# Two projections side by side, rope tables and squared sums on DVE, and shifted due times in a two-block Transformer kernel

## The chip, the core and the metric

The kernel runs on one core of a Trainium2 chip. The metric is the device time of one execution in microseconds (us). PE is the matrix engine (TensorE), DVE the vector engine (VectorE), ACT the scalar engine (ScalarE), POOL is GpSimd, SP the engine that issues most of the DMAs.

## The reference

The input is one sequence of 256 tokens of width 1024, in fp32. Two blocks follow each other.

The first block puts 16 meta tokens ahead of the sequence (272 tokens), normalizes (RMS), projects, runs two kinds of attention, and then a gated FFN of width 2816. Cut to what matters here:

```python
h = rms_norm(x, attn_norm_g)
qa, ka, va, qb, kb, vb = split(h @ w_in)     # A: 8 query heads, 2 key heads of 64; B: 4 x 2 heads
qa = apply_rope(rms_norm(qa, a_q_norm_g), ang_a)
ka = apply_rope(rms_norm(ka, a_k_norm_g), ang_a)
out_a = softmax(qa ka^T / 8) va
out_b = rms_norm((softmax_0 - lam * softmax_1) vb, subln_g)
x = x + concat(out_a, out_b) @ w_out
x = x + (silu(h2 @ w_gate) * (h2 @ w_up)) @ w_down
```

The second block has a gated spatial MLP, a dilated window attention in three groups, a merge of both, and an FFN of width 4096 with a squared ReLU. The change touches its instructions only through the planner's order.

## The kernel before

**Precision by splitting.** Every fp32 operand of a matmul is held as two parts, `hi` (rounded to fp32r) and `lo` (the rest), and a product is made of three matmuls: hi x hi, hi x lo, lo x hi. ACT writes `hi` with a copy, DVE writes `lo` with a subtraction. Weights come as chunks of 128x1024 fp32 (512 KB) in the order of use. `Weights` loads them into four raw buffers (`wraw`), splits them into six pairs `whi`, `wlo` (`fill`, one ACT copy and one DVE subtraction for each chunk, called a chunk split below; the first chunk is split in two halves of 512 columns), and issues the next load behind each split. The hidden state of the first block is `hx` (128 partitions, 8 slices of 128 features, hi and lo, 272 tokens), made at the start from `xT`, the transposed input: for each slice k an ACT copy scaled by the norm's gain column and a DVE multiply-and-subtract.

**Projections of the first block.** There are 18 (`P1`, each through `proj`): kA, qA0, vA, qA1 to qA3, and k, q, v of the four B heads. One takes one chunk: for each k two matmuls (whi with hi and lo of `hx`), then eight with wlo. With q and k follow a square on ACT (for the norm), and `rotate`: a shuffle and a product with a cosine table on DVE, a product with a sine table on POOL, an addition on DVE. The eight tables (cos and sin for q and k of A and B, 128x272 each) are rope values times gain columns, made at the start by eight POOL `tensor_scalar` instructions. `token_sums` adds up the squares of x over the slices (seven POOL additions of 128x272) and makes from them the terms of the norms (`msx`, `emx`, `rx`). Powers of -1/2 run on POOL. Then come scores, softmax, transposes and products with v (`SA`, `TA`, `VA`, `SB`, `TB`, `VB`), and the output projection (`WO`).

**The order of the work.** `Recorder` doesn't issue at once. It notes each instruction with its dependences and a price in ns (`price`), and `flush` runs a list scheduler over them: each engine takes, of the instructions that are ready, the one with the earliest due time. Due times come from a target per PE instruction, handed back through the dependences. Six rounds are made, each with the times of the one before as targets, and the order with the earliest end of PE is issued. Each engine then runs its queue in this fixed order. There are two flushes: one after the first block's FFN has reached feature tile f6, one at the end. As all instructions are issued in `flush`, the profile gives all of them line 422.

**The start.** PE runs nine warm-up matmuls on zeros. SP issues the loads in the order of `FIRST`: x slices 0 and 1, `cols` (34 columns, among them the eight gain columns of the norm), the first chunk's first half, x slices 2 and 3, its second half, the rest of x, then chunks, `ind`, `rope`, `ident`, `lam`.

Of the kernel before, what the change touches and what calls it, by code (L numbers as in the profile page):

```python
# [19 lines left out]
T = 256  # L20
# [201 lines left out]
ISSUE, FETCH, LAND = 470.0, 1100.0, 950.0  # L222
# [4 lines left out]
def late(a, b):  # L227
    return LAND if a == "sync" else LATE.get((a, b), 150.0)
# [6 lines left out]
class Recorder:  # L235


    def __init__(self, tc, nc):
        self.tc, self.nc = tc, nc
        self.ops, self.acc, self.label, self.next = [], {}, "", set()  # L240
        self.clock = {e: 0.0 for e in ("tensor", "vector", "scalar", "gpsimd", "sync")}

    def engine(self, name):
        rec, eng = self, getattr(self.nc, name)

        class Proxy:
# [4 lines left out]

    def add(self, eng, m, fn, args, kw):
# [11 lines left out]
        o.cost = self.price(eng, m, outs, ins, kw)  # L264
# [43 lines left out]
    def price(self, eng, m, outs, ins, kw):  # L308
# [35 lines left out]
        return 100.0 + 1.43 * n * int(list(outs[0].ap)[0][1]) / 128.0  # L344

    def schedule(self, target):
# [16 lines left out]
        moved, bank = 0.0, {}  # L363
# [3 lines left out]
        while len(order) < len(ops):  # L367
# [29 lines left out]
            for j in o.succ:  # L397
                ready[j] = max(ready[j], clock[e] if e == ops[j].eng == "sync" else end + late(e, ops[j].eng))
# [5 lines left out]
    def flush(self):  # L404
# [45 lines left out]
class Weights:  # L450
# [56 lines left out]
def build(tc, a, out):  # L507
# [7 lines left out]
    V, S, G, PE, DMA = (R.engine(n) for n in ("vector", "scalar", "gpsimd", "tensor", "sync"))  # L515
# [11 lines left out]
    cols = top.tile([128, 34], F32, name="cols")  # L527
# [4 lines left out]
    hx = top.tile([128, 8, 2, L], F32R, name="hx")  # L532
# [176 lines left out]
    xT = prob[:, : 8 * L].rearrange("p (k q) -> p k q", k=8)  # L709
# [13 lines left out]
    for step in FIRST:  # L723
        R.follow()
        if step[0] == "x":
            ks = slice(int(step[1]), int(step[2]))
            DMA.dma_start(xT[:, ks], a["xT"][:, ks])
        elif step == "c":
            DMA.dma_start(cols, a["cols"])
        elif step == "w":  # L730
            W.load()
        else:
            W.load_part(int(step[1]))
    R.follow()
    DMA.dma_start(ind, a["ind"])
    R.follow()
    DMA.dma_start(rope, a["rope1"])
    R.follow()
    DMA.dma_start(ident, a["ident"])
    R.follow()  # L740
    DMA.dma_start(lamv, bass.AP(tensor=a["lam"].tensor, offset=a["lam"].offset, ap=[[0, 128], [64, 4], [1, 64]]))
# [880 lines left out]
```

## Time and profile before

| | |
|---|---|
| median of 3 runs | 739.33 us (738.82 to 739.93) |
| the profiled execution | 738.85 us, its span 737.1 us |
| granted clock of PE, mean | 0.992 of 2.4 GHz |
| busy share of PE, DVE, ACT, POOL | 98%, 73%, 59%, 9% |
| read from HBM | 130 MB, 178 GB/s over the span |

The span runs from the first instruction to the last. Busy times count instructions at work, not waits; a matmul's end is modelled, so neighbours overlap in the rows, and the distance from start to start is the better measure. The granted clock is a share of 2.4 GHz: 1.00 is the upper level, 0.50 the lower one of 1.2 GHz. A row of a timeline merges like instructions that follow each other; in brackets stands how long the engine had idled before, and what ended it.

### The profile page before, as it was taken

Reading aid. Unit: us, or ns where it says so; the run is one execution under the profiler, and the core shown is the slowest. Engines: PE = TensorE matmul, PEld = TensorE weight load, DVE = VectorE, ACT = ScalarE, POOL = GpSimd, SP = SyncE. Lnnn points to the kernel's source line nnn. Section 1 sums busy time; section 2 is a strip of 40 time slices with the busy share of each in tenths; the row PEclk is TensorE's granted clock in tenths of the full one; section 3 lists DMA queues with packets and bytes.
Section 4 is the critical chain, followed back from the end, with each engine's and each line's share of the span. In section 5 each row is a group of like instructions: output and inputs, shape, how many; then the busy total and the mean of one; then the engine's idle time right before and its main releaser. Section 6 shows DMA issues by size and latency. Waiting matters only on the chain.

```text
span 737.1 us, 11095 instructions
## 1 busy us (share of the span) xinstructions
PE 723.6 (98%) x4085; PEld 625.3 (85%) x4085; DVE 539.0 (73%) x944; ACT 431.3 (59%) x779; POOL 67.9 (9%) x81
## 2 busy tenths in 40 slices
PE   8989999999999999999999999999999999999996
PEld 5989988888888888888888889888888888888885
DVE  6897986666666665678748999757999766666663
ACT  6697775655555545466646766656656544454441
POOL 5932230100000000010000000000130000000000
PEclk8999999999999999999999999999999999999998
DMA  8553314466865565547655444545646755555621
GB/s 286 166 194 122 136 58 144 143 204 229 296 197 182 191 196 195 181 142 255 215 187 177 157 153 138 171 159 191 194 149 192 251 190 195 194 190 189 197 89 57
DMA packets 37639, 131.85 MB, mean 179 GB/s; under 512 B 4432, under 2 KB 5200, under 8 KB 37584
## 3 DMA queue, kind: packets, MB, share of 16 engines
q1 hardware_dynamic: 37584, 131.14, 53.8%
q8 instruction: 32, 0.52, 0.3%
q14 instruction: 23, 0.19, 0.1%
HBM read 130.07 MB, written 1.05 MB: 178 GB/s over the span
## 4 chain that ended last, share of the span: by engine, by line
PE 89%; DVE 5%; ACT 3%; issue 1%; DMA 1%; SPq 0%; POOLq 0%; POOL 0%; DVEq 0%; ACTq 0%
PE bank L422 89%; DVE wlo L422 2%; ACT prob L422 1%; DVE tiny L422 1%; DMA prob<-in_xT_dram 1%; ACT whi L422 1%; DVE ro L422 0%; DVE ptl L422 0%; DVE qkf L422 0%; DVE rr L422 0%; ACT hx L422 0%; DVE q L422 0%; ACT L422 0%; ACT vhiA L422 0%; SPq L422 0%
## 5 line engine op out<-in xcount | busy, mean ns | idle before, releaser
L422 DVE TENSOR_TENSOR wlo<-wraw,whi 128x1024 fp32r<-128x1024 f32 (+1 forms) x235 | 286.9, 1225 | 117.6 <-ACT whi L422 115.6
L422 ACT ACTIVATE whi<-wraw 128x1024 fp32r<-128x1024 f32 (+1 forms) x235 | 245.3, 1052 | 126.9 <-issue 73.4
L422 PE MATMUL bank<-hx,whi 128*128 128x512 f32 (+2 forms) x1152 | 270.2, 370 | 3.7 <-DVE ptl L422 1.1
L422 PEld LDWEIGHTS bank<-hx,whi 128*128 128x128 f32 x1152 | 196.2, 190 | 34.8 <-ACT whi L422 1.9
L422 PE MATMUL bank<-whi,mix 128*128 128x512 f32 x496 | 154.9, 392 | 0.0
L422 PEld LDWEIGHTS bank<-hx,wlo 128*128 128x128 f32 x1008 | 136.7, 189 | 9.5
L422 PE MATMUL bank<-hx,wlo 128*128 128x256 f32 (+1 forms) x1008 | 141.8, 283 | 0.0
L422 PEld LDWEIGHTS bank<-whi,mix 128*128 128x128 f32 x496 | 92.9, 188 | 17.1
L422 PE MATMUL bank<-wlo,mix 128*128 128x512 f32 x248 | 96.2, 391 | 0.0
L422 PE MATMUL bank<-whi,hx 128*128 128x512 f32 x288 | 91.6, 397 | 0.0
L422 PEld LDWEIGHTS bank<-whi,hx 128*128 128x128 f32 x288 | 54.0, 188 | 12.2
L422 PE MATMUL bank<-wlo,hx 128*128 128x512 f32 x144 | 56.2, 396 | 0.0
L422 PEld LDWEIGHTS bank<-wlo,mix 128*128 128x128 f32 x248 | 46.6, 188 | 9.2
L422 ACT ACTIVATE scr<-bank 128x256 f32<-128x256 f32 x64 | 24.0, 375 | 48.8 <-PE bank L422 48.7
L422 POOL TENSOR_TENSOR tiny<-tiny,half 128x1 f32<-128x1 f32 (+1 forms) x15 | 14.8, 989 | 405.5 <-DVE tiny L422 405.2
L422 DVE TENSOR_TENSOR scr<-bank,scr 128x256 f32<-128x256 f32 x64 | 27.0, 422 | 26.5 <-ACT scr L422 26.5
L422 PEld LDWEIGHTS bank<-wlo,hx 128*128 128x128 f32 x144 | 27.1, 188 | 6.4 <-DVE wlo L422 0.4
L422 ACT ACTIVATE prob<-bank,tiny,rq 128x272 f32<-128x272 f32 x32 | 18.1, 575 | 10.1 <-DVE tiny L422 10.1
L422 POOL TENSOR_TENSOR gates<-xres,gains 128x1024 f32<-128x1024 f32 x2 | 5.0, 2506 | 193.7 <-ACT hx L422 180.8
L422 PE MATMUL bank<-mix,whi 128*128 128x512 f32 x64 | 21.6, 397 | 0.0
L422 ACT ACTIVATE qkf<-bank 128x256 f32<-128x256 f32 x28 | 10.5, 376 | 17.6 <-PE bank L422 17.5
L422 DVE TENSOR_TENSOR mix<-scr,mix 128x256 fp32r<-128x256 f32 x46 | 19.3, 419 | 0.5 <-ACT mix L422 0.5
(213 smaller groups left out, 706.1 us busy)
## 6 DMA issues: line engine op xcount, KB each, us to landing
wraw<-in_w_dram SPq DMA_DIRECT2D x233, 512.0 KB, 3.4
prob<-in_xT_dram SPq DMA_DIRECT2D x4, 272.0 KB, 4.7
xres<-in_x_dram SPq DMA_DIRECT2D x2, 512.0 KB, 4.4
rope<-in_rope_dram SPq DMA_DIRECT2D x1, 544.0 KB, 7.8
wraw<-in_w_dram SPq DMA_DIRECT2D x2, 256.0 KB, 4.3
gains<-in_ffn_norm_g_dram SPq DMA_DIRECT2D x1, 512.0 KB, 4.2
gains<-in_norm_mix_pre_dram SPq DMA_DIRECT2D x1, 512.0 KB, 4.6
qkf<-in_ln_dram SPq DMA_DIRECT2D x1, 512.0 KB, 5.2
```

The costliest lines, as they stand in the source:

```text
L422: o.fn(*o.args, **o.kw)
```

## The change

- Two projections side by side. A new task `PP` makes kA and qA0 together. Their two chunks are packed anew (`in0:0`, `in0:1`): the first holds slices 0 to 3 of both, the second slices 4 to 7. For each k, six matmuls: whi with hi and lo for both projections, then wlo with hi for both. All other projections come behind `PP`.
- Loads. The gains of the first norm travel in the first eight columns of `xT`; `cols` shrinks to 26 columns and is loaded later. Both of the first chunks are loaded and split in halves. The halves of the first are issued from ACT's queue (`early`), all else from SP's in a new order.
- `hx` lies in a buffer that has two views: one with 272 tokens (first block's projections) and one with 256 tokens, in which hi and lo of a slice adjoin (all later uses).
- The eight tables and the seven additions of the squares run on DVE.
- The planner: prices of DVE, ACT and POOL are multiplied by 1.04; loads start 1.9 us late in its model (`RAMP`) and have new prices; after the six rounds, one more schedule is made with the best round's targets shifted by a number of ns per task (`SHIFT`, some 80 entries for the first flush, none for the second), and the better by the model is issued.

```diff
+ABREAST = ("kA", "qA0")
...
+    p.add("PP", 5.8, [], [f"in0:{j}" for j in range(2)], prio=999)
     for i, f in enumerate(fts):
-        p.add("P" + f, 2.7, [], ["in:" + f], prio=1000 + i)
+        if f in ABREAST:
+            p.add("P" + f, 0.0, [("PP", 0.0)], [], prio=1000 + i)
+        else:
+            p.add("P" + f, 2.7, [("PP", 0.0)], ["in:" + f], prio=1000 + i)
...
-FIRST = ("x02", "c", "h0", "x24", "h1", "x46", "x68", "w", "w", "w")
+MARGIN = 1.04
+FIRST = dict(
+    early=("h00", "h01"),
+    sync=("x01", "x12", "x24", "x46", "h10", "x68", "h11", "c", "w", "rope", "ind", "ident", "w", "lam"),
+)
...
+SHIFT = (
+    {"WO0": -2702, "V1B0": -4028, "N1B2": -5894, "K1B2": 7979, "f4": -17708, "Q1B1": 35704, "K1B1": -3155,
...
+    {},
+)
...
-ISSUE, FETCH, LAND = 470.0, 1100.0, 950.0
+ISSUE, FETCH, LAND, RAMP = 470.0, 1100.0, 950.0, 1900.0
+QUEUES = dict(sync="sync", early="scalar")
...
-        o.cost = self.price(eng, m, outs, ins, kw)
+        o.cost = self.price(eng, m, outs, ins, kw) * (MARGIN if eng in ("vector", "scalar", "gpsimd") else 1.0)
...
-        return 100.0 + 1.43 * n * int(list(outs[0].ap)[0][1]) / 128.0
+        return 60.0 + 1.27 * n * int(list(outs[0].ap)[0][1]) / 128.0
...
-        moved, bank = 0.0, {}
+        moved, bank = RAMP, {}
...
-                best = order, at, clock
+                best, base = (order, at, clock), target
             target = [at[o.i] + o.cost if o.eng == "tensor" else 1e18 for o in ops]
+        part, self.part = SHIFT[self.part], self.part + 1
+        best = min(best, self.schedule([t + part.get(o.label, 0) for t, o in zip(base, ops)]), key=lambda b: b[2]["tensor"])
...
-            n = 1024 if self.ready else 512
+            n = 512 if self.ready < self.halves else 1024
...
-    hx = top.tile([128, 8, 2, L], F32R, name="hx")
+    hbuf = top.tile([128, 16 * L], F32R, name="hx")
+    hxm = hbuf.rearrange("p (k a q) -> p k a q", k=8, a=2)
+    hx = hbuf[:, : 16 * T].rearrange("p (k a q) -> p k a q", k=8, a=2)
...
-    xT = prob[:, : 8 * L].rearrange("p (k q) -> p k q", k=8)
+    xg = prob[:, :8]
+    xT = prob[:, 8 : 8 + 8 * L].rearrange("p (k q) -> p k q", k=8)
...
     for k in range(8):
-        g = cols[:, 26 + k : 27 + k]
-        hlast = S.activation(hh[:, k], xT[:, k], AF.Copy, scale=g)
-        V.scalar_tensor_tensor(hl[:, k], xT[:, k], g, hh[:, k].bitcast(F32), op0=ALU.mult, op1=ALU.subtract)
+        g = xg[:, k : k + 1]
+        hlast = S.activation(hxm[:, k, 0], xT[:, k], AF.Copy, scale=g)
+        V.scalar_tensor_tensor(hxm[:, k, 1], xT[:, k], g, hxm[:, k, 0].bitcast(F32), op0=ALU.mult, op1=ALU.subtract)
...
-        G.tensor_scalar(tab["c" + c], rope[:, u], cols[:, 2 * i : 2 * i + 1], 0.0, op0=ALU.mult, op1=ALU.add)
-        G.tensor_scalar(tab["s" + c], rope[:, u + 1], cols[:, 2 * i + 1 : 2 * i + 2], 0.0, op0=ALU.mult, op1=ALU.add)
+        V.tensor_scalar(tab["c" + c], rope[:, u], cols[:, 2 * i : 2 * i + 1], 0.0, op0=ALU.mult, op1=ALU.add)
+        V.tensor_scalar(tab["s" + c], rope[:, u + 1], cols[:, 2 * i + 1 : 2 * i + 2], 0.0, op0=ALU.mult, op1=ALU.add)
...
+    def PP():
+        bks = [B.get() for _ in ABREAST]
+        ns = [T if f[0] == "q" else L for f in ABREAST]
+        for k in range(8):
+            wh, wl = W.get(f"in0:{k // 4}")
+            cs = [slice(256 * (k % 4) + 128 * i, 256 * (k % 4) + 128 * i + 128) for i in range(2)]
+            for bk, n, c in zip(bks, ns, cs):
+                mm(bk[:, :n], wh[:, c], hxm[:, k, 0, :n], k == 0, False)
+                mm(bk[:, :n], wh[:, c], hxm[:, k, 1, :n], False, False)
+            for bk, n, c in zip(bks, ns, cs):
+                mm(bk[:, :n], wl[:, c], hxm[:, k, 0, :n], False, k == 7)
+            if k % 4 == 3:
+                W.done(f"in0:{k // 4}")
...
-        bk = proj("in:" + f, hh, hl, n)
+        bk = st.pop("g" + f) if f in ABREAST else proj("in:" + f, hxm[:, :, 0], hxm[:, :, 1], n)
...
-                G.tensor_tensor(sqx[:, :L], sqx[:, :L], s, op=ALU.add)
+                V.tensor_tensor(sqx[:, :L], sqx[:, :L], s, op=ALU.add)
```

## Rows read from the trace of the kernel before

**Rows 1.** The page's busy times: engine, share of the span, instructions.

```profile
PE 723.6 (98%) x4085; PEld 625.3 (85%) x4085; DVE 539.0 (73%) x944; ACT 431.3 (59%) x779; POOL 67.9 (9%) x81
```

**Rows 2.** Stretches: length, busy us of PE, PEld, DVE, ACT, POOL; clock, DMA, GB/s.

```profile
5.20:9.60 4.40, 2.36 (x10) 1.41 (x10) 2.95 (x8) 3.61 (x9) 0.00 (x0) 0.95 1.03 354
9.60:16.00 6.40, 6.09 (x25) 5.66 (x26) 4.87 (x8) 5.12 (x11) 5.63 (x6) 0.50 1.02 378
11.30:18.30 7.00, 6.96 (x41) 6.96 (x42) 5.53 (x10) 4.25 (x10) 6.76 (x6) 0.67 0.90 319
18.30:76.40 58.10, 55.14 (x462) 52.51 (x461) 49.71 (x135) 45.10 (x109) 29.29 (x33) 1.00 0.47 160
30.00:60.00 30.00, 27.88 (x236) 26.14 (x236) 29.37 (x75) 23.98 (x60) 13.91 (x15) 1.00 0.46 159
76.40:140.00 63.60, 63.58 (x435) 56.17 (x435) 51.97 (x131) 42.69 (x103) 14.45 (x16) 1.00 0.34 115
76.40:730.80 654.40, 653.70 (x3563) 562.26 (x3563) 475.36 (x779) 373.21 (x645) 27.47 (x26) 1.00 0.54 178
```

**Rows 3.** The chain of waits, where it stays on PE: start, length, what.

```profile
76.37 23.28 PE bank L422 x197
```

**Rows 4.** PE's timeline of the start: start us, length, instructions, count.

```profile
6.21 0.77 PE L422 MATMUL bank<-hx,whi 128*128 128x272 f32 x4 [1.02 <-ACT whi L422]
...
17.72 0.73 PE L422 MATMUL bank<-ind,sq 128*128 128x2 f32 x6
18.30 2.25 PE L422 MATMUL bank<-hx,whi 128*128 128x272 f32 x16
20.39 1.17 PE L422 MATMUL bank<-hx,wlo 128*128 128x272 f32 x8
21.40 0.72 PE L422 MATMUL bank<-ones,gains 128*128 128x2 f32 x6
```

**Rows 5.** ACT's and DVE's timeline of the start, the same columns.

```profile
5.53 0.63 ACT L422 ACTIVATE whi<-wraw 128x512 fp32r<-128x512 f32 x1 [0.71 <-DMA wraw<-in_w_dram]
...
8.43 0.69 DVE L422 TENSOR_TENSOR wlo<-wraw,whi 128x512 fp32r<-128x512 f32 x1
...
9.04 2.25 DVE L422 SCALAR_TENSOR_TENSOR hx<-prob,cols,hx 128x272 fp32r<-128x272 f32 x4
...
16.33 1.20 DVE L422 TENSOR_TENSOR wlo<-wraw,whi 128x1024 fp32r<-128x1024 f32 x1
```

**Rows 6.** DMA: one issue on SP, and GB/s of the first 12 us.

```profile
1.63 0.42 SPq L422 DMA_DIRECT2D wraw<-in_w_dram  x1
...
GB/s 0 0 0 0 0 44 131 181 380 255 228 218 89 70 239 270 349 320 321 402 353 359 354 290 353 307 311 323 363 431 369 437 396 396 437 410 437 423 388 384
```

**Rows 7.** POOL, two of its timeline, then its moved work by groups.

```profile
17.78 0.76 POOL L422 TENSOR_TENSOR gains<-gains 128x272 f32<-128x272 f32 x1
...
18.52 0.49 POOL L422 TENSOR_SCALAR rope<-rope,cols 128x272 f32<-128x272 f32 x1
...
L422 POOL TENSOR_TENSOR gains<-gains 128x272 f32<-128x272 f32 x7 | 6.5, 925 | 7.1 <-ACT gains L422 6.8
...
L422 POOL TENSOR_SCALAR tabq<-rope,cols 128x272 f32<-128x272 f32 x4 | 5.0, 1242 | 0.0
...
L422 POOL TENSOR_SCALAR rope<-rope,cols 128x272 f32<-128x272 f32 x4 | 3.3, 822 | 0.1
```

**Rows 8.** DVE's groups of the first 76.4 us, then one of all.

```profile
L422 DVE TENSOR_TENSOR wlo<-wraw,whi 128x1024 fp32r<-128x1024 f32 x17 | 22.3, 1313 | 0.9 <-ACT whi L422 0.9
...
L422 DVE TENSOR_TENSOR rr<-ro,ro 128x272 f32<-128x272 f32 x3 | 1.3, 424 | 0.0
...
L422 DVE TENSOR_SCALAR prob<-prob,tiny 128x512 f32<-128x512 f32 x8 | 3.8, 484 | 0.2
```

**Rows 9.** PE's groups from 140 to 400 us (moving operand, then weights).

```profile
L422 PE MATMUL bank<-hx,whi 128*128 128x512 f32 x383 | 98.9, 392 | 0.0
...
L422 PE MATMUL bank<-whi,mix 128*128 128x512 f32 x176 | 53.7, 390 | 0.0
```

More of the change, by code (lines that the diff above doesn't have):

```diff
@@ L239, in __init__ @@
         self.tc, self.nc = tc, nc
-        self.ops, self.acc, self.label, self.next = [], {}, "", set()
-        self.clock = {e: 0.0 for e in ("tensor", "vector", "scalar", "gpsimd", "sync")}
+        self.ops, self.acc, self.label, self.next, self.part = [], {}, "", set(), 0
+        self.clock = {e: 0.0 for e in ("tensor", "vector", "scalar", "gpsimd", *QUEUES)}
     def engine(self, name):
-        rec, eng = self, getattr(self.nc, name)
+        rec, eng = self, getattr(self.nc, QUEUES.get(name, name))
         class Proxy:
@@ L352, in schedule @@
             for j in o.succ:
-                d = min(d, due[j] - ops[j].cost - late(o.eng, ops[j].eng) - (FETCH if ops[j].eng == "sync" else 0.0))
+                d = min(d, due[j] - ops[j].cost - late(o.eng, ops[j].eng) - (FETCH if ops[j].eng in QUEUES else 0.0))
             due[o.i] = d
@@ L397, in schedule @@
             for j in o.succ:
-                ready[j] = max(ready[j], clock[e] if e == ops[j].eng == "sync" else end + late(e, ops[j].eng))
+                ready[j] = max(ready[j], clock[e] if e == ops[j].eng and e in QUEUES else end + late(e, ops[j].eng))
                 left[j] -= 1
@@ L467, in load, with load_part @@
             self.loaded += 1
-    def load_part(self, h):
+    def load_part(self, i, h, q):
         cs = slice(512 * h, 512 * h + 512)
-        self.dma.dma_start(self.raw[0][:, cs], self.dram[0][:, cs])
-        self.loaded = 1
+        q.dma_start(self.raw[i][:, cs], self.dram[i][:, cs])
+        self.loaded = self.halves = i + 1
     def fill(self):
@@ L514, in build @@
     B = Banks(psum)
-    V, S, G, PE, DMA = (R.engine(n) for n in ("vector", "scalar", "gpsimd", "tensor", "sync"))
+    V, S, G, PE, DMA, EARLY = (R.engine(n) for n in ("vector", "scalar", "gpsimd", "tensor", "sync", "early"))
     def mm(o, l, r, first, last):
@@ L526, in build @@
     ident = top.tile([128, 128], F32, name="ident")
-    cols = top.tile([128, 34], F32, name="cols")
+    cols = top.tile([128, 26], F32, name="cols")
     ind = top.tile([128, 2], F32, name="ind")
@@ L722, in build @@
     G.memset(sqx[:, L:], 0.0)
[L723 to L741, printed above, removed]
+    for q, steps in FIRST.items():
+        for i, step in enumerate(steps):
+            if i:
+                R.follow()
+            if step[0] == "x":
+                cs = slice(8 + L * int(step[1]) if step[1] != "0" else 0, 8 + L * int(step[2]))
+                dict(sync=DMA, early=EARLY)[q].dma_start(prob[:, cs], a["xT"][:, cs])
+            elif step == "c":
+                DMA.dma_start(cols, a["cols"])
+            elif step == "w":
+                W.load()
+            elif step[0] == "h":
+                W.load_part(int(step[1]), int(step[2]), dict(sync=DMA, early=EARLY)[q])
+            elif step == "ind":
+                DMA.dma_start(ind, a["ind"])
+            elif step == "rope":
+                DMA.dma_start(rope, a["rope1"])
+            elif step == "ident":
+                DMA.dma_start(ident, a["ident"])
+            elif step == "lam":
+                DMA.dma_start(lamv, bass.AP(tensor=a["lam"].tensor, offset=a["lam"].offset, ap=[[0, 128], [64, 4], [1, 64]]))
     for k in range(8):
-        g = cols[:, 26 + k : 27 + k]
-        hlast = S.activation(hh[:, k], xT[:, k], AF.Copy, scale=g)
-        V.scalar_tensor_tensor(hl[:, k], xT[:, k], g, hh[:, k].bitcast(F32), op0=ALU.mult, op1=ALU.subtract)
+        g = xg[:, k : k + 1]
+        hlast = S.activation(hxm[:, k, 0], xT[:, k], AF.Copy, scale=g)
+        V.scalar_tensor_tensor(hxm[:, k, 1], xT[:, k], g, hxm[:, k, 0].bitcast(F32), op0=ALU.mult, op1=ALU.subtract)
     W.fill()
@@ L799, in rotate @@
         return r
+    def PP():
[11 more added lines that the diff above has]
+                W.done(f"in0:{k // 4}")
+        for f, bk in zip(ABREAST, bks):
+            st["g" + f] = bk
     def P1(f):
@@ L1104, in build @@
             WO(int(n[2:]))
+        elif n == "PP":
+            PP()
         elif n[0] == "P":
@@ L1533, in chunk @@
             return ft(w_in, cols_in(r))
+        if kind == "in0":
+            ks = [slice(128 * k, 128 * k + 128) for k in range(4 * int(r), 4 * int(r) + 4)]
+            return np.concatenate([w_in[k][:, cols_in(f)] for k in ks for f in ABREAST], axis=1)
         if kind == "out1":
@@ L1578, in _pack @@
         w[j] = chunk(n)
-    cols = np.zeros((128, 34), np.float32)
+    cols = np.zeros((128, 26), np.float32)
     sw = np.arange(64) ^ 1
@@ L1586, in _pack @@
     cols[:, 10:26] = g["b_gate_2"][0].reshape(16, 128).T
-    cols[:, 26:34] = g["attn_norm_g"][0].reshape(8, 128).T
     x = np.concatenate([g["x"][0][pos], g["meta_tokens"]])
@@ L1590, in _pack @@
         x=x[:T].reshape(2, 128, D),
-        xT=x.T.reshape(8, 128, L).transpose(1, 0, 2),
+        xT=np.concatenate(
+            [g["attn_norm_g"][0].reshape(8, 128).T, x.T.reshape(8, 128, L).transpose(1, 0, 2).reshape(128, 8 * L)], axis=1
+        ),
         w=w,
```

4 lines of the change are left out of this document (2 added, 2 removed), and 13 rows, old and new, of the table SHIFT.

## The prediction

> **What bounds the kernel now.** I began with the page's busy shares [rows 1]: PE is busy for 723.6 of 737.1 us, so a change that leaves the matmuls alone can take off no more than the 13.5 us in which PE idles, and what PE loses at a low clock. The table by stretches shows where that is [rows 2]. From 76.4 to 730.8 us PE idles for 0.7 us in all; only the first 76 us and the last 6.3 us, in which no matmul is left, have holes. The change doesn't touch the end. So the question is when PE gets through its first stretch, and the chain of waits agrees: from 76.37 us on it goes through PE [rows 3]. Every us by which PE comes earlier to its state at 76.4 us is a us off the end, as long as the later stage goes on as it is.
>
> In that stretch there are two separate losses. Up to 18.3 us PE is short of data. After its warm-up matmuls it waits for the first split weights until 6.21 us [rows 4], and from 5.2 to 9.6 us it is busy for 2.36 of 4.40 us. Then, from 9.6 to 16.0 us, it runs at a granted clock of 0.50, the 1.2 GHz level [rows 2]. From 18.3 to 76.4 us PE idles for 58.10 - 55.14 = 2.96 us, and DVE is busy for 49.71 of the 58.10 us, between 30 and 60 us for 29.37 of 30 [rows 2]. There DVE sets the pace.
>
> **The start, step by step.** Before, projections kA and qA0 follow each other: when DVE has split the last piece of the hidden state, at 9.04 + 2.25 = 11.3 us [rows 5], nearly half of kA's 24 matmuls and all of qA0's still stand before PE. They and six small matmuls last until 18.30 us [rows 4]. After, each slice k serves both projections at once: PE has twice the work per slice that has come, and behind the last slice only that slice's own six matmuls are left.
>
> When is the last slice there? The new order needs all of x and two whole weight chunks, 1.1 + 1.0 = 2.1 MB, ahead of it (before: x and one chunk). The GB/s line of the first 12 us, 0.3 us to a slice, sums to 2.1 MB at 9.0 us [rows 6]; transfers overlap, so I allow 0.7 us for the last one: 9.7 us. Its split as a half chunk takes 0.63 us on ACT and 0.69 us on DVE [rows 5], to 11.0. A 272-column matmul takes 0.126 us from start to start (eight from 20.39 to 21.40 [rows 4]), so the last two slices, twelve matmuls, are 1.5 us, partly beside the splits. I take 12.3 us as the end of both projections. Bounds: the 48 matmuls by themselves are 6.0 us, and the warm-up ends at 5.2 (6.21 less the 1.02 us of waiting [rows 4]), so 11.2 us is the earliest. At the latest, DVE's last piece ends where it does now, the two added half chunks come wholly behind it (1.4 us), then 1.5 us: 14.2 us. Before, the same point is 18.30 us less the 0.58 us from 17.72 us on for the small matmuls [rows 4], which now come later: 17.7 us. So the start gives 5.4 us, between 3.5 and 6.5.
>
> Two DMA issues (h00, h01) move from SP's queue, where one takes 0.42 us [rows 6], to ACT's. If the second stands there behind the table load, it is late by 1 to 2 us, still before its slice (k = 2) is wanted, after 6.5 us: nothing, at most 0.5 us. cols moves behind the x pieces, rope behind the next two weight chunks: rope is there after 3.2 MB, about 12 us [rows 6], and POOL was still at its tables at 18.52 us [rows 7]. The third chunk is there after 2.6 MB, 10.5 us, and split by 12 to 13 us: PE may wait for it, 0 to 0.5 us.
>
> **What DVE gets to do.** The seven sums: a DVE addition of this shape takes 424 ns [rows 8], 3.0 us. The eight tables: no such DVE instruction of this shape is in the trace. The nearest, a 128x512 multiply by a column, takes 484 ns [rows 8]; scaled to 272 columns 0.26 us, unscaled 0.48 us, so 2.1 to 3.9 us. I take 2.2 us, since it is nearly all time per column. Together 5.2 us (5.1 to 6.9). Something comes back: beside POOL's early work a chunk split on DVE takes longer, 1313 ns on the mean of 17 in the first 76 us [rows 8] against 1.20 us [rows 5], 1.9 us in all. POOL keeps its rope products and powers, so I credit 1.2 us. Net 4.0 us more on DVE (3.2 to 6.9).
>
> Does that fit? Before, from 11.3 to 76.4 us DVE was busy for 5.53 + 49.71 us [rows 2]. With 4.0 it is 59.2 us of work between 12.3 and 76.4 - 5.4 = 71.0 us, which has 58.7 us. DVE would have to run without a hole, where it had 8.4 us of holes. What helps is that chunk splits for later can be put off: from 76.4 to 140 us DVE idles for 11.6 us [rows 2]. I charge 0.6 us for what doesn't fit.
>
> POOL loses 14.8 us of sums and tables [rows 7], so that the powers of the norms, queued behind them, can start earlier, and attention with them. That gives the list scheduler more to choose from; I price it at nothing, bounded by PE's 2.96 us of idle.
>
> **Orders.** The margin of 1.04, RAMP, the new DMA prices and the shifts add no instruction. In the second flush only the margin and these prices act; nearly all of the 0.7 us of holes after 76.4 us could go, or another hole of 1 us come: 0, from -0.6 to +1.0. The closed-up hx makes a moving operand of two 256-column pieces contiguous: such matmuls take 392 ns, others with a contiguous operand of 512 columns 390 [rows 9]: nothing; 864 x 2 ns = 1.7 us at the very most.
>
> **Sum**, against the profiled execution of 738.85 us (span 737.1), which lies 0.5 us below the median of 739.33, inside the spread of the runs: -5.4 at the start, +0.6 on DVE, together -4.8: 734.0 us.
>
> **Rivals.**
> (a) DVE takes half back. If DVE keeps 2.5 us of its 8.4 us of holes and nothing is put off, PE comes to its state of 76.4 us at 12.3 + 59.2 + 2.5 = 74.0 us: 736.5 us. For it: DVE's 29.37 of 30 us. Against: 7.8 us of its holes lie outside that stretch, where orders can be changed.
> (b) Slower. DVE keeps all 8.4 us of holes (waits for ACT's and PE's results in its own fixed queue) and PE waits for its splits: 12.3 + 59.2 + 8.4 = 79.9 us, 3.5 us later than now: 742.4 us. It decides from 76.4 - 12.3 - 59.2 = 4.9 us of kept holes on. Against it: before, DVE's 8.4 us of holes went with only 2.96 us of PE's.
> (c) The clock falls again. If PE is still too often idle between 5.2 and 9.6 us, it runs at 0.50 up to 16 us as now; 6.09 busy us [rows 2] at half speed are 3.0 us lost: 737.0 us. Against: it has twice the work per slice there.
> (d) DVE wins by the move. The moved instructions kept POOL busy for 6.5 + 5.0 + 3.3 us; undisturbed they take 0.76 us (seven) and 0.49 us (eight), 9.2 us; for the other 5.6 us they stood against DVE [rows 7]. If DVE stood as long for them, the net load is 5.2 - 5.6 = -0.4 us, everything fits, and PE's 2.96 us go too: 738.85 - 5.4 - 3.0 = 730.5 us. The trace bears it out only in part: 1.9 us on DVE's chunk splits. The Trainium skill, "SBUF — State Buffer", section "Who interferes with whom", has this as a rule: a DVE instruction with two SBUF inputs and a GpSimd instruction that reads SBUF exclude each other for a whole instruction. By that rule (d) is the expected case; the tables' mean of 1.24 us on POOL against 0.49 us undisturbed agrees with it [rows 7].
> (e) The change does not do what it says, and the first matmuls still wait for one projection after the other: 738.9 us.
>
> **Numbers.** Forecast 0.60, (a) 0.12, (b) 0.06, (c) 0.08, (d) 0.11, (e) 0.03. The forecast's own range is 732 to 736. The range 730.4 to 737.2 takes in (a), (c), (d) and the bounds of the start; (b), (e) and the tails stay out. A difference of 0.2%, 1.5 us, is about what a measurement of this kernel can tell from no change. Faster 0.87 (a part of (c) ends within it), same 0.06, slower 0.07.
>
> **What would show it.** Right: the clock is at 1.00 through 9.6 to 16 us; vA's first matmul starts near 12.3 us in place of 18.3; POOL has no 128x272 sums or tables; DVE is over 95% busy from 12 to 70 us; PE's last hole of the first stage ends near 71 us; from there to the end the rows are as now. Wrong: vA starts at 12 to 13 us, but PE has over 5 us of holes up to 75 us that end on DVE (a, b); a clock of 0.50 in the first 16 us (c); chunk splits at 1.20 us and hardly a hole on PE (d); new PE holes after 140 us, by which the second flush's orders were not free.

## The result, and the profile after

The changed kernel takes 733.47 us (median of 4 runs, 732.71 to 734.51) against 739.25 us: a ratio of 0.9925, 95% interval 0.9912 to 0.9938. That is 5.8 us less where 4.8 to 5.3 were forecast (734.0 against 738.85 and 739.33 us). The time was right; the experiments below show that the path by which I got there was not.

The page's busy times of the kernel after, to set beside [rows 1]:

```profile
span 731.5 us, 11081 instructions
...
PE 721.8 (99%) x4085; PEld 626.1 (86%) x4085; DVE 537.9 (74%) x960; ACT 431.9 (59%) x780; POOL 63.6 (9%) x66
```

Of the 5.6 us of span, PE's idle time gave 3.8 us (13.5 to 9.7) and its busy time 1.8 us. The table by stretches of the kernel after (length, busy us of PE, PEld, DVE, ACT, POOL, then clock, DMA share, GB/s) answers to [rows 2]:

```profile
5.20:9.60 4.40, 4.40 (x30) 4.20 (x30) 4.25 (x9) 4.33 (x11) 0.00 (x0) 1.00 1.04 383
9.60:16.00 6.40, 6.40 (x54) 6.40 (x54) 6.37 (x20) 5.47 (x13) 0.72 (x1) 1.00 1.02 377
16.00:20.00 4.00, 3.17 (x26) 2.88 (x25) 3.57 (x14) 3.23 (x5) 2.70 (x5) 0.99 0.47 175
20.00:23.30 3.30, 3.30 (x18) 3.30 (x17) 2.19 (x5) 1.33 (x5) 3.14 (x4) 0.50 0.45 139
30.00:60.00 30.00, 29.47 (x246) 27.25 (x246) 29.10 (x82) 27.25 (x67) 13.23 (x12) 1.00 0.50 166
```

From 5.2 to 16 us it is as forecast: PE is busy throughout, at full clock. New is a stretch at half clock from 20.0 to 23.3 us. PE's timeline shows what came before it; the brackets hold the wait ahead of the row:

```profile
11.72 0.41 PE L459 MATMUL bank<-hx,wlo 128*128 128x272 f32 x2
11.96 1.04 PE L459 MATMUL bank<-hx,whi 128*128 128x272 f32 x7
...
16.79 0.83 PE L459 MATMUL bank<-ones,gains 128*128 128x2 f32 x6 [0.18 <-DVE gains L459]
18.26 0.38 PE L459 MATMUL bank<-ones,gains 128*128 128x2 f32 x2 [0.64 <-POOL gains L459]
...
29.89 0.39 PE L459 MATMUL bank<-khiA,q 64*128 64x272 f32 x2
```

The third projection (vA) starts at 11.96 us, where [rows 4] have 18.30. Then PE stands twice ahead of the sums' small matmuls, for DVE and for two copies on POOL. The first score matmul (khiA, q) is at 29.89 us. Before, it was this one:

```profile
33.49 0.40 PE L422 MATMUL bank<-khiA,q 64*128 64x272 f32 x2
```

In the end PE is through 5.4 us earlier, though it was 6.3 us ahead at vA.

DVE's groups of the first 71 us, against [rows 8], and two groups of the moved work:

```profile
L459 DVE TENSOR_TENSOR wlo<-wraw,whi 128x1024 fp32r<-128x1024 f32 x15 | 19.9, 1330 | 0.0
...
L459 DVE TENSOR_TENSOR gains<-gains 128x272 f32<-128x272 f32 x7 | 3.1, 437 | 0.0
...
L459 DVE TENSOR_SCALAR tabq<-rope,cols 128x272 f32<-128x272 f32 x4 | 1.4, 350 | 0.0
```

The sums take 437 ns and the tables about 350 ns, 5.9 us together (taken: 5.2, bounds 5.1 to 6.9). A chunk split takes 1330 ns on the mean, not less than the 1313 before: what I credited for DVE and POOL no longer standing against each other did not come on the splits.

### The profile page after: what moved, and what is told of

The parts are those of the page before. It is cut to its first block, busy times and chain, and to the rows that moved or that the text cites. A ratio compares the mean times of both kernels' runs of the same rounds, so it can differ in the third digit from the quotient of the medians.

```text
span 731.5 us, 11081 instructions
## 1 busy us (share of the span) xinstructions
PE 721.8 (99%) x4085; PEld 626.1 (86%) x4085; DVE 537.9 (74%) x960; ACT 431.9 (59%) x780; POOL 63.6 (9%) x66
## 4 chain that ended last, share of the span: by engine, by line
PE 88%; DVE 5%; ACT 2%; issue 2%; POOL 1%; DMA 1%; SPq 0%; POOLq 0%; DVEq 0%; ACTq 0%
PE bank L459 88%; DVE wlo L459 1%; DVE tiny L459 1%; ACT prob L459 1%; DMA prob<-in_xT_dram 1%; DVE ro L459 1%; POOL ro L459 0%; DVE ptl L459 0%; DVE rr L459 0%; ACT whi L459 0%; SPq L459 0%; DVE gains L459 0%; ACT pth L459 0%; POOL gains L459 0%; ACT sq L459 0%
## 5 line engine op out<-in xcount | busy, mean ns | idle before, releaser
L459 PE MATMUL bank<-hx,whi 128*128 128x512 f32 (+2 forms) x1152 | 279.6, 370 | 0.0
L459 PEld LDWEIGHTS bank<-hx,whi 128*128 128x128 f32 x1152 | 199.4, 190 | 30.2 <-ACT whi L459 0.9
L459 PE MATMUL bank<-hx,wlo 128*128 128x256 f32 (+1 forms) x1008 | 150.2, 285 | 0.0
L459 PEld LDWEIGHTS bank<-hx,wlo 128*128 128x128 f32 x1008 | 141.5, 191 | 9.5 <-issue 0.2
L459 ACT ACTIVATE mix<-scr 128x256 fp32r<-128x256 f32 x46 | 18.8, 409 | 6.8 <-DVE scr L459 6.7
L459 DVE TENSOR_TENSOR mix<-scr,mix 128x256 fp32r<-128x256 f32 x46 | 19.3, 419 | 1.5 <-ACT mix L459 1.5
```

The source lines that it names most:

```text
L459: o.fn(*o.args, **o.kw)
```

## The experiments

The first runs put three explanations against each other; the expectations use their letters. **S**: the earlier start is the gain (the forecast). **L**: it is the move off POOL, since DVE and POOL stop standing against each other (rival d). **O**: the shifted due times do it. Ratios are to the kernel before.

**The start alone.** From the changed kernel:

```diff
-MARGIN = 1.04
+MARGIN = 1.0
-SHIFT = ({"WO0": -2702,
...
+SHIFT = ({}, {})
-        V.tensor_scalar(tab["c" + c], rope[:, u], cols[:, 2 * i : 2 * i + 1], 0.0, op0=ALU.mult, op1=ALU.add)
+        G.tensor_scalar(tab["c" + c], rope[:, u], cols[:, 2 * i : 2 * i + 1], 0.0, op0=ALU.mult, op1=ALU.add)
...
-                V.tensor_tensor(sqx[:, :L], sqx[:, :L], s, op=ALU.add)
+                G.tensor_tensor(sqx[:, :L], sqx[:, :L], s, op=ALU.add)
```

> The changed kernel with the eight tables and seven sums back on POOL, without the shifts and with the margin at 1.0: what is left is the start (two projections side by side, the loads, the two views of hx, the load prices). Theory S (the start is the gain, as predicted: 5.4 us, DVE's share about nothing): 733.5 to 735.5 us. Theory L (DVE and POOL stop standing against each other, 2 to 3 us of the gain): 736 to 737.5 us. Theory O (the shifted due times are what turns the earlier start into time): 736 us or more.

Measured: 744.96 us, ratio 1.0079 (1.0063 to 1.0094): slower than before. S and L fall; O's range (736 us or more) takes it in, but O speaks of a gain that needs the shifts, not of a loss of 5.8 us. Yet the start itself did what it should. PE's timeline of this kernel, then POOL's:

```profile
14.10 2.16 PE L443 MATMUL bank<-hx,whi 128*128 128x272 f32 x16
...
23.35 0.83 PE L443 MATMUL bank<-ones,gains 128*128 128x2 f32 x6 [1.14 <-POOL gains L443]
...
25.71 0.38 PE L443 MATMUL bank<-ones,gains 128*128 128x2 f32 x2 [0.95 <-POOL gains L443]
...
32.26 0.90 PE L443 MATMUL bank<-ident,rw 128*128 128x128 f32 x3 [2.74 <-POOL rw L443]
...
37.82 0.40 PE L443 MATMUL bank<-khiA,q 64*128 64x272 f32 x2
```

```profile
12.94 1.52 POOL L443 TENSOR_SCALAR tabq<-rope,cols 128x272 f32<-128x272 f32 x1 [0.53 <-ACT gains L443]
...
20.84 1.74 POOL L443 TENSOR_TENSOR ro<-ro,rope 128x272 f32<-128x272 f32 x1
22.54 0.76 POOL L443 TENSOR_TENSOR gains<-gains 128x272 f32<-128x272 f32 x1
...
24.13 1.53 POOL L443 COPY gains<-gains 128x16 f32<-128x16 f32 x2
...
31.70 0.50 POOL L443 COPY rw<-tiny 128x384 f32<-128x384 f32 x1
```

The last of POOL's sums in the kernel before:

```profile
18.97 0.78 POOL L422 TENSOR_TENSOR gains<-gains 128x272 f32<-128x272 f32 x1
```

vA starts at 14.10 us, 4.2 us earlier than before. But the last sum is done on POOL at 23.3 us (before: 18.97 + 0.78 = 19.75), since tables and rope products, for which rope is there sooner (12.8 us, before 14.4), stand between the sums. PE runs out of work and waits in its own queue for POOL: 1.14, 0.95 and 2.74 us. The first scores come at 37.8 us in place of 33.5, and PE then runs at a mean clock of 0.90 between 30 and 100 us. So I formed theory **C**: the chain from the sums over POOL's powers and copies (`rx`, `tiny`, `rw`) to the first scores sets the pace of the first stage. PE's lead over it is worth nothing, since nothing else is left to do, and each stand can cost the clock as well.

**The move alone.**

```diff
-        G.tensor_scalar(tab["c" + c], rope[:, u], cols[:, 2 * i : 2 * i + 1], 0.0, op0=ALU.mult, op1=ALU.add)
+        V.tensor_scalar(tab["c" + c], rope[:, u], cols[:, 2 * i : 2 * i + 1], 0.0, op0=ALU.mult, op1=ALU.add)
...
-                G.tensor_tensor(sqx[:, :L], sqx[:, :L], s, op=ALU.add)
+                V.tensor_tensor(sqx[:, :L], sqx[:, :L], s, op=ALU.add)
```

> The kernel before with the eight tables and the seven sums on DVE and nothing else changed. Theory S: within 1 us of before, 738.3 to 740.3 us, since PE is short of data up to 18 us anyway. Theory L: 2 to 3 us faster, 736.5 to 737.5 us. A DVE that is simply overloaded would be 1 to 3 us slower, 740.5 to 742.5 us.

Measured: 736.27 us, 0.9965 (0.9952 to 0.9979): 2.9 us faster, about what L says (2 to 3 us; its range ends at 736.5). But its first scores are at 29.79 us, 3.7 us earlier than before, which L doesn't need and C does. Its stretch from 9.6 to 16 us kept the full clock, too, and vA began at 16.61 us; how much of the 2.9 us is due to that was not separated:

```profile
29.79 0.40 PE L422 MATMUL bank<-khiA,q 64*128 64x272 f32 x2
```

```profile
5.20:9.60 4.40, 3.07 (x11) 2.46 (x11) 3.10 (x8) 3.72 (x8) 0.00 (x0) 1.00 1.01 338
9.60:16.00 6.40, 6.40 (x39) 6.31 (x39) 5.51 (x12) 5.34 (x11) 0.00 (x0) 1.00 1.03 383
```

**Everything but the move.** The tables' and sums' lines of the changed kernel go back to POOL; the start, the margin and the shifts stay.

```diff
-        V.tensor_scalar(tab["c" + c], rope[:, u], cols[:, 2 * i : 2 * i + 1], 0.0, op0=ALU.mult, op1=ALU.add)
+        G.tensor_scalar(tab["c" + c], rope[:, u], cols[:, 2 * i : 2 * i + 1], 0.0, op0=ALU.mult, op1=ALU.add)
...
-                V.tensor_tensor(sqx[:, :L], sqx[:, :L], s, op=ALU.add)
+                G.tensor_tensor(sqx[:, :L], sqx[:, :L], s, op=ALU.add)
```

> The changed kernel with the eight tables and the seven sums back on POOL; margin and shifts stay. Theory S: 733 to 734.5 us. Theory L: 735.5 to 737 us. The shifts were made for another set of instructions, so an extra hole of up to 1 us on PE would not speak for L unless it ends on POOL.

Measured: 741.06 us, 1.0023 (1.0013 to 1.0033), above the ranges of S and of L. The move is worth 7.6 us here, against 2.9 us on the kernel before. First scores at 39.5 us, the latest of all.

**Without the shifts**, all else as changed.

```diff
-SHIFT = ({"WO0": -2702,
...
+SHIFT = ({}, {})
```

> The changed kernel without the shifts (both tables empty), margin kept. Theory S: within 1 us of the changed kernel, 732.5 to 734.5 us. Theory O: 735.5 us or more, with PE holes between 12 and 80 us of over 4 us in place of 2.4 us.

Measured: 735.30 us, 0.9949 (0.9935 to 0.9963). The shifts are worth about 1.8 us, between S and O, but only just clear of the noise: the two intervals overlap at their ends, and from both together the difference lies anywhere between about 0.4 and 3.2 us. PE's idle time from 5.2 to 140 us is 6.1 us without them, 2.4 us with them.

**Is it only the planner's wrong POOL prices?** To the first kernel:

```diff
+            if m == "tensor_scalar":
+                return 1030.0
+            if m == "tensor_copy" and n < 64:
+                return 690.0
             return 200.0 + 1.0 * n
```

> start_only (745.0 us), with two of the planner's POOL prices set to what the traces show: a table 1.03 us in place of 0.47, a 16-column copy 0.69 us in place of 0.22. No instruction is added or taken out; only the orders change. Theory C (POOL's chain from the sums over the powers to the first scores sets when attention starts, and PE has no other work for that long): 743 us or more, the first score matmul still after 36 us. Theory P (PE stands in start_only because the planner put its matmuls in an order that POOL, slower than priced, can't keep): 739 us or less, PE's waits for POOL gone.

Measured: 743.77 us, 1.0063 (1.0048 to 1.0078); first scores at 39.4 us. PE's waits named POOL for 0.9 us only, but it stood for ACT and DVE results of the same chain instead. C holds, P falls, for these two prices.

**Only the sums on DVE.** The run without shifts, with the two table lines back on POOL as well:

```diff
-        V.tensor_scalar(tab["c" + c], rope[:, u], cols[:, 2 * i : 2 * i + 1], 0.0, op0=ALU.mult, op1=ALU.add)
+        G.tensor_scalar(tab["c" + c], rope[:, u], cols[:, 2 * i : 2 * i + 1], 0.0, op0=ALU.mult, op1=ALU.add)
```

> The changed kernel without shifts (735.3 us), with only the tables back on POOL; the seven sums stay on DVE. Theory C: the sums head the chain, the tables only share POOL's queue with it: 735 to 737.5 us, the first score matmul by 32 us. If the tables matter as much as the sums: 738 us or more. If it is DVE's load alone that counts: faster than 735 us, since DVE gets 2.8 us less to do.

Measured: 741.31 us, 1.0025 (1.0013 to 1.0038): 6.0 us more than with the tables on DVE, a miss of my expectation. POOL's timeline, and PE's wait behind it:

```profile
12.92 1.88 POOL L443 TENSOR_SCALAR tabq<-rope,cols 128x272 f32<-128x272 f32 x2 [9.68 <-DMA rope<-in_rope_dram]
...
19.36 1.94 POOL L443 TENSOR_SCALAR rope<-rope,cols 128x272 f32<-128x272 f32 x2
...
21.93 0.57 POOL L443 COPY gains<-gains 128x16 f32<-128x16 f32 x2
```

```profile
22.55 0.59 PE L443 MATMUL bank<-ones,gains 128*128 128x2 f32 x2 [2.44 <-POOL gains L443]
```

```profile
18.34 0.42 DVE L443 TENSOR_TENSOR gains<-gains 128x272 f32<-128x272 f32 x1
```

This is DVE's last sum, done at 18.8 us, but the two small copies that close them stand in POOL's queue behind all eight tables. PE stands 2.44 us, and from 24 to 30 us its clock is 0.61.

**The same with the two copies on DVE.** In addition to the edit above:

```diff
-            G.tensor_copy(sqx[:, L + 32 * j : L + 32 * j + NM], sqx[:, T:L])
+            V.tensor_copy(sqx[:, L + 32 * j : L + 32 * j + NM], sqx[:, T:L])
```

> sums_on_dve (741.3 us; no shifts, tables on POOL) with the two 16-column copies on DVE. Theory C, with POOL's queue as the place: in sums_on_dve the copies stood behind eight tables until 21.93 us and PE 2.44 us behind them, so that with the copies out of POOL's queue it is 735.5 to 738 us. If it is the tables' own lateness (the rotations wait for them) or their standing against DVE: 740 us or more.

Measured: 736.48 us, 0.9958 (0.9946 to 0.9970). With the two copies of 16 columns out of that queue the kernel is 4.8 us faster (the planner orders the stage anew here, as in every run). The other 1.2 us, to the 735.30 us with the tables on DVE, are not clear of the noise (the two intervals overlap), and that run has its copies on POOL: what the tables' place as such is worth is not shown.

**A longer chain and nothing else.**

```diff
         V.tensor_scalar(msx, bk[:, 0:8:2], EPS, None, op0=ALU.add)
         B.put(bk)
+        for j in range(3):
+            R.follow()
+            G.memset(scr.t[0], 0.0)
+        R.follow()
         V.tensor_scalar(emx.rearrange("p (j i) -> p j i", j=3), msx[:, :3, None].to_broadcast([128, 3, 2]), EPS, None, op0=ALU.mult)
```

> The changed kernel (733.5 us) with three added POOL memsets of 128x1024, about 1 us each, in the chain between the sums' result and the term of the norms that every key norm waits for (they write a scratch tile that nothing reads yet). DVE, ACT and PE get nothing more to do. Theory C (the chain from the sums to the first scores sets the pace, PE runs out of other work): the first score matmul moves from 29.9 to 32 us or later, 735.5 to 738.5 us. If PE has enough projections to fill in: 734 us or less.

Measured: 742.44 us, 1.0051 (1.0037 to 1.0066): 9.0 us more than the changed kernel for 2.8 us of POOL work. PE's timeline:

```profile
27.44 3.69 PE L459 MATMUL bank<-hx,whi 128*128 128x272 f32 x16 [1.58 <-DVE ro L459]
...
33.09 0.55 PE L459 MATMUL bank<-ident,rw 128*128 128x128 f32 x3 [0.97 <-POOL rw L459]
35.24 1.92 PE L459 MATMUL bank<-hx,whi 128*128 128x256 f32 x14 [1.60 <-DVE rr L459]
37.09 0.40 PE L459 MATMUL bank<-khiA,q 64*128 64x272 f32 x2
```

The first scores move by 7.2 us. PE doesn't fill in: it stands, and sixteen matmuls at 27.44 us take 3.69 us, at a clock of 0.57 from 27.4 to 31.2 us. The direction is what C says; the size is over its range. The added work is short, but rope products and other chain links queue behind it on POOL and DVE, and the planner's order changed around it; what share each has was not separated. The ten executions differ as well: two with a mean clock of 0.994 and 0.995 take 740.2 us, the eight with 0.986 to 0.991 take 742.2 to 744.8 us.

**kA's matmuls ahead of qA0's.** In the new task, the loop over the two projections goes outside and the loop over k inside (the weight buffers then come free behind qA0's matmuls):

```diff
-        for k in range(8):
+        for i, (bk, n) in enumerate(zip(bks, ns)):
+            for k in range(8):
...
```

> The changed kernel with the same loads and halves, but kA's 24 matmuls ahead of qA0's 24 in the new task. If it is the work per slice that makes the start: behind the last slice stand 3 + 24 matmuls in place of 6, 2.6 us more, the third projection starts near 14.6 us in place of 12.0, and the time is 735 to 737 us. Theory C in its strong form (only the norm chain counts, the projections have slack): 734 us or less.

Measured: 733.71 us, 0.9924 (0.9909 to 0.9939). As a test of the order it is inconclusive: the planner put the matmuls side by side again, as they are ready side by side. But this run says something else. A wait for a weight split holds PE up at 9.76 us, vA starts 2.2 us later than in the changed kernel, and the first scores come at 29.89 us all the same, to the hundredth:

```profile
14.18 1.75 PE L459 MATMUL bank<-hx,whi 128*128 128x272 f32 x12
...
19.32 0.38 PE L459 MATMUL bank<-ones,gains 128*128 128x2 f32 x2 [0.64 <-POOL gains L459]
```

```profile
20.00:23.30 3.30, 3.30 (x32) 3.30 (x30) 3.30 (x9) 1.46 (x6) 3.30 (x4) 1.00 0.48 159
```

PE has the same stand of 0.64 us behind POOL's copies as in the changed kernel, and no fall of the clock after it. Its last matmul starts 0.1 us later than that of the changed kernel, whose clock fell.

So the order was then forced:

```diff
+                if i and not k:
+                    R.follow(last)
                 mm(bk[:, :n], wh[:, c], hxm[:, k, 0, :n], k == 0, False)
...
-                mm(bk[:, :n], wl[:, c], hxm[:, k, 0, :n], False, k == 7)
+                last = mm(bk[:, :n], wl[:, c], hxm[:, k, 0, :n], False, k == 7)
```

> As serial_pair, where the planner had put the two projections' matmuls side by side again because they are ready side by side; now qA0's first matmul is tied behind kA's last. If the work per slice makes the start: the third projection starts near 14.6 us in place of 12.0, and the time is 734.5 to 737 us. If the chain of the norms alone counts, 734 us or less, as kA comes no later.

Measured: 732.72 us, 0.9911 (0.9892 to 0.9929), no slower than the changed kernel. PE's timeline of this kernel:

```profile
12.59 0.43 PE L459 MATMUL bank<-hx,wlo 128*128 128x272 f32 x1
12.82 0.63 PE L459 MATMUL bank<-hx,whi 128*128 128x256 f32 x2
...
16.18 2.17 PE L459 MATMUL bank<-hx,whi 128*128 128x272 f32 x16
...
30.39 0.40 PE L459 MATMUL bank<-khiA,q 64*128 64x272 f32 x2
```

kA ends at about 12.8 us, qA0 only at 16.2 us: vA starts 4.2 us later than in the changed kernel, after holes and a mean clock of 0.73 from 9.6 to 16 us. The first scores are 0.5 us later, and the time is not worse. This speaks most plainly against S: PE's place at 12 us is no measure of the end.

**Start and move without shifts or margin.** All else as changed.

```diff
-MARGIN = 1.04
+MARGIN = 1.0
-SHIFT = ({"WO0": -2702,
...
+SHIFT = ({}, {})
```

> The start and the move together with nothing of the planner's numbers: no shifts, margin 1.0. If the two parts simply add up (start alone +5.9 us, move alone -2.9 us), 742 us. Theory C (the earlier start is worth something only once the chain is off POOL): 734.5 to 737 us. Against no_shift (735.3 us) it gives the margin's own part.

Measured: 735.03 us, 0.9942 (0.9921 to 0.9963). The parts don't add up (that would be 742 us): the start costs 5.8 us without the move (744.96 against 739.13 in its comparison). On top of the move no cost is seen; whether it brings anything there is not shown, as 736.27 and 735.03 us have intervals that overlap. The executions fall into two groups: three with a mean clock of 0.997 to 0.999 take 733.4 to 733.6 us, as the changed kernel does, three with 0.993 take 736.4 to 736.6 us. So the median goes with how often the clock fell. The margin's own part can't be told from nothing in the time (735.30 with it), but one row shows it at work. The stretch from 400 to 430 us of this kernel, then of the changed one:

```profile
400.00:430.00 30.00, 29.36 (x186) 26.24 (x185) 27.41 (x62) 21.13 (x41) 0.00 (x0) 1.00 0.47 153
```

```profile
400.00:430.00 30.00, 30.00 (x190) 26.94 (x190) 27.56 (x61) 21.64 (x43) 0.00 (x0) 1.00 0.46 146
```

PE's hole of 0.6 us there is in the kernel before and in the runs with the margin at 1.0, and in none that has 1.04.

**The copies on DVE in the changed kernel.**

```diff
-            G.tensor_copy(sqx[:, L + 32 * j : L + 32 * j + NM], sqx[:, T:L])
+            V.tensor_copy(sqx[:, L + 32 * j : L + 32 * j + NM], sqx[:, T:L])
```

> The changed kernel (733.5 us) with the two 16-column copies that close the sums on DVE in place of POOL, where they took 1.33 us and PE stood behind them for 0.64 us and then ran at half clock from 20 to 23.3 us. Theory C: 731.5 to 733 us, no PE wait for POOL before 20 us, and a clock of 1.00 from 20 to 24 us if that stand was what dropped it. If the orders decide more than the chain: anywhere from 732.5 to 735 us, as the shifts were made with the copies on POOL.

Measured: 732.79 us, 0.9913 (0.9899 to 0.9928). The two stretches that mattered, in this kernel:

```profile
16.00:20.00 4.00, 3.81 (x33) 3.61 (x33) 4.00 (x15) 3.27 (x5) 1.94 (x2) 1.00 0.68 235
20.00:23.30 3.30, 3.30 (x29) 3.13 (x28) 3.30 (x9) 2.12 (x6) 3.30 (x3) 1.00 0.05 15
23.30:30.00 6.70, 5.71 (x49) 4.98 (x48) 6.45 (x22) 4.39 (x10) 4.38 (x6) 1.00 0.60 185
```

PE is busy for 3.81 of 4.00 us before 20 us (changed kernel: 3.17), and the clock stays at 1.00 in the stretch where it fell to 0.50, as the expectation has it; since it stayed up behind the same stand of 0.64 us in the run with kA first, not forced, too, the stand is not shown to be what dropped it. Then a hole of 1.0 us comes after 23.3 us (6.70 - 5.71; changed kernel: 0.47). The first score matmul is at 28.96 us, 0.9 us earlier. In time it can't be told apart from the changed kernel, as the intervals overlap (0.9899 to 0.9928 against 0.9912 to 0.9938). This run and the forced order are the lowest of the study, and both are faster than the kernel before; that either beats the changed kernel is not shown.

## Why the prediction was right or wrong, point by point

One sum over the traces ties the runs together. From 5.2 to 140 us, in 27 stretches of at most 6.7 us, I add up what PE loses: its idle time (length less PE's busy time), and its busy time times (1 - granted clock). In us:

| kernel | median | span | idle | low clock | lost | span less lost |
|---|---|---|---|---|---|---|
| forced order | 732.72 | 731.4 | 2.8 | 1.7 | 4.5 | 726.9 |
| copies on DVE | 732.79 | 730.8 | 3.4 | 0.0 | 3.4 | 727.4 |
| changed | 733.47 | 731.5 | 2.4 | 1.7 | 4.1 | 727.4 |
| kA first, not forced | 733.71 | 731.6 | 3.8 | 0.0 | 3.8 | 727.8 |
| no shifts, margin 1.0 | 735.03 | 731.6 | 3.4 | 0.0 | 3.4 | 728.2 |
| no shifts | 735.30 | 733.3 | 6.0 | 1.5 | 7.5 | 725.8 |
| move alone | 736.27 | 734.2 | 3.1 | 0.0 | 3.1 | 731.1 |
| sums and copies on DVE | 736.48 | 736.1 | 3.9 | 4.7 | 8.6 | 727.5 |
| before | 739.25 | 737.1 | 5.3 | 3.2 | 8.5 | 728.6 |
| no move | 741.06 | 738.9 | 8.0 | 4.6 | 12.6 | 726.3 |
| sums on DVE | 741.31 | 740.7 | 7.1 | 7.2 | 14.3 | 726.4 |
| longer chain | 742.44 | 738.5 | 9.0 | 2.4 | 11.4 | 727.1 |
| start, POOL priced | 743.77 | 742.7 | 7.9 | 6.1 | 14.1 | 728.6 |
| start alone | 744.96 | 743.3 | 8.5 | 5.7 | 14.2 | 729.1 |

Spans differ by 12.5 us, what is left by 3.3 us, but for the move alone, whose 731.1 us has 2.0 us or more that this sum doesn't find. (The spans are of one execution each and lie 0.4 to 3.9 us below the medians.)

One caution with the column of the low clock. 43 executions of the kernel before are on record beside its profile, each with its mean clock. Ten have 0.997 to 0.999 and take 738.5 to 739.7 us. Of the 25 at 0.992 to 0.995, twenty take 738.4 to 739.3 us and five 740.5 to 740.8; the eight at 0.990 and 0.991 take 739.1 to 741.2 us. Where the clock fell in them is not recorded. But down to 0.992, the profiled execution's own value, the usual time doesn't change, so that the 3.2 us that it lost at 0.50 can't be counted as 3.2 us at its end. These executions all have one and the same order of the work.

**Right: where the time is.** The step "only the first 76 us and the last 6.3 us ... have holes", and that a us gained there is a us off the end, held. Of the 5.6 us of span, 4.4 are the difference of what PE lost (8.5 to 4.1), and rows after 140 us are as before, but for the hole at 400 to 430 us, priced at 0 within -0.6 to +1.0, which closed for 0.6 us. The last hole of the first stage is not near 71 us, as forecast, but at 82.7 us, 0.55 us behind DVE's `vT`.

**Right: the sizes of the parts.** Both projections end at 11.96 us (forecast 12.3, bounds 11.2 to 14.2). The clock is at 1.00 from 9.6 to 16 us. The added DVE work is 5.9 us (taken 5.2, within 5.1 to 6.9; the tables take 2.8 us, where 2.2 were taken as if nearly all of it went by the column), and DVE fits it in: busy for 29.10 of 30 us between 30 and 60 us, 29.37 before, and for 92% from 12 to 70 us, where over 95% were named as the sign. The 8.4 us of DVE holes in the forecast are those from 18.3 us on; over the stretch that it reckons with, from 11.3 us, there are 9.9 us (1.47 + 8.39, [rows 2]), by which (b) would be 743.9 us. PE's holes between 30 and 76.4 us shrink from 2.71 (46.40 - 43.69) to 0.53 us (46.40 - 45.87).

**Wrong: the step "So the start gives 5.4 us".** The lead at vA is real, 6.3 us, but it was put down as a gain at the end, and by itself it is none: the start alone has 4.2 us of it and is 5.8 us slower than before; the forced order gives 4.2 us of it away and loses nothing. The sum of lost time alone would not tell: in the first 16 us PE loses 5.5 us before and nothing in the changed kernel, just the forecast's number, and after them 3.0 and 4.1 us. But the start alone also cuts the first part, to 1.0 us, and then loses 13.2 us behind it, and the forced order loses 3.0 us in the first part and 1.5 us behind it for the same time. I had looked at what PE waits for up to 18 us and taken the wait that ended last there for the path. The path was beside it, on DVE and POOL: sums, two copies, two powers, `rw`, then the first scores. What PE has left to do in advance of them is limited, and a PE that is ahead stands later, in part at a lower clock.

**Wrong: the step that prices POOL's early chain at nothing.** The text says that the powers "can start earlier, and attention with them", and then bounds it by PE's 2.96 us of idle. That is no bound: with the chain left on POOL behind an earlier start, holes and low clock grow. The move is worth 2.9 us alone and 7.6 us in the changed kernel; two 16-column copies in the wrong queue are worth 4.8 us; 2.8 us put into the chain cost 9.0 us. That the time came out right is luck: the sum has 5.4 us for a start that brings nothing by itself and nothing for the chain and the shifts, and no run shows why their sum should be the start's 5.4 us. The time of the first scores tells the slowest kernels from the fastest: 34.8 us or later in the five slowest, 28.8 to 30.4 us in eight of the faster ones, among which it does not order them. The two between don't fit as well: 33.5 us in the kernel before (739.25 us), but 33.2 us in the run with sums and copies on DVE, which with 736.48 us is as fast as the move alone with 29.8 us.

**Wrong: the credit of 1.2 us for chunk splits, and rival (d).** Splits stay at 1330 ns (1313 before, 1200 for one alone), so nothing came back on them. The traces show why. In the kernel before, two splits took 0.8 us longer between them beside POOL's sums, at 11.51 us (1.49 us) and at 14.63 us; the other long ones stood beside work that stays on POOL. In the changed kernel most take 1.20 to 1.23 us and four 1.62 to 1.74 us, and each of these four begins during a rope product on POOL. A split before, then such a product and the split behind it after:

```profile
14.63 1.75 DVE L422 TENSOR_TENSOR wlo<-wraw,whi 128x1024 fp32r<-128x1024 f32 x1
```

```profile
35.09 0.73 POOL L459 TENSOR_TENSOR ro<-ro,tabq 128x256 f32<-128x256 f32 x1
```

```profile
35.17 1.74 DVE L459 TENSOR_TENSOR wlo<-wraw,whi 128x1024 fp32r<-128x1024 f32 x1
```

Rival (d), at 730.5 us, supposed that DVE had stood for the moved work as long as that stood for DVE, 5.6 us; on the splits it was 0.8 us. The Trainium skill's rule in "SBUF — State Buffer", section "Who interferes with whom", is the one by which (d) was the expected case. These rows agree with it on who stands for whom, as do four of the moved tables, 1242 ns on the mean on POOL against 0.49 us undisturbed [rows 7]; the step from there to equal stands on both sides is what did not hold. DVE's busy time on the page still falls by 1.1 us in spite of the 5.9 us added, for a reason far from the change: at 520 to 543 us, beside POOL's 128x1024 products, three DVE instructions of 128x256 took 2.55 to 2.63 us each before, where others take 0.41 us. After, one does (at 516 us), and one of the POOL products takes 8.07 us instead. PE has no hole there in either kernel.

**Orders.** I took the shifts' net effect as 0; they are worth about 1.8 us (735.30 to 733.47, just clear of the noise). PE's idle time in the first stage falls by more, 6.0 to 2.4 us, so the two don't match. The margin's effect is a closed hole of 0.6 us, not told apart in the time. What rival (c) feared came in another place: the clock fell not in the first 16 us, but from 20.0 to 23.3 us. Its price of 3.0 us is not borne out: the executions of the kernel before are no faster at 0.997 than at 0.992.

**Open.** Why a chain longer by 2.8 us costs 9.0 us: the planner's order changed as well. How much of the move alone is the unfallen clock (its sum loses 3.2 us less there, all that it gains; the executions of the kernel before speak against so much). Whether the early issue on ACT's queue matters, and what the loads' new prices and `RAMP` or the two views of `hx` do: none was tried by itself, and all of them are in the start alone. How much of each difference is the planner's new order and not the edit: only the executions of one kernel are free of that.

## What to carry to other kernels

Before a wait is priced as a gain, follow the work behind it to the next point where every engine must meet (here the first scores), and ask which chain reaches that point last; an earlier start on another engine is then worth nothing until that chain is shorter. Look at the small instructions of such a chain and at what stands ahead of them in their in-order queue, rather than at the busy share of the engine: POOL was busy for 9% of the span and held up the first scores. And try the parts of a change alone and left out: here they don't add up (+5.8 and -2.9 us make -4.1 us).

## What the runs showed of the hardware

PE's stands ahead of the half clock were short. In the changed kernel they are 0.18 and 0.64 us, between two-column matmuls, at 16.8 and 18.3 us, and the granted clock is 0.99 from 16 to 20 us, then 0.50 from 20.0 to 23.3 us. With the forced order, whose PE is busy for all of 16 to 23.3 us, it is 1.00 there; with the copies on DVE, where the one stand before 20 us is 0.19 us, also. But in the run with kA first, not forced, it is 1.00 as well, behind a stand of 0.64 us at 19.3 us. So these stands alone don't tell when the clock falls.

The same small instruction on POOL has no fixed price, and what DVE does beside it has a part in that. The two copies in the changed kernel, with DVE's chunk split beside them, then the copies in the move alone:

```profile
16.88 1.33 POOL L459 COPY gains<-gains 128x16 f32<-128x16 f32 x2 [0.58 <-DVE gains L459]
...
19.91 1.64 POOL L459 TENSOR_TENSOR tiny<-tiny,half 128x6 f32<-128x6 f32 x1
```

```profile
16.93 1.22 DVE L459 TENSOR_TENSOR wlo<-wraw,whi 128x1024 fp32r<-128x1024 f32 x1
```

```profile
18.45 0.46 POOL L422 COPY gains<-gains 128x16 f32<-128x16 f32 x2 [15.24 <-DVE gains L422]
```

They take 1.33 us in the one and 0.46 us in the other. Of the twelve kernels with the copies on POOL, six have a chunk split running on DVE at that time, and there the pair takes 1.31 to 1.55 us; in the other six it takes 0.33 to 0.57 us. By these numbers, PE's 0.64 us behind the copies in the changed kernel would go with another place for that one split. A power of 128x6 elements takes 1.64 us there, more than twice a 128x272 sum on POOL (0.76 us, [rows 7]); a split runs beside most of it, too (from 20.27 us).
